# A two-layer encoder on one Trainium2 core: the split weights of each column block are placed at one of twelve odd shifts in their tiles

## The chip, the cores and the metric

The kernel runs on one core of one Trainium2 chip. The metric is the device time of one execution in microseconds (us), the median over runs. Five engines work side by side and meet only at semaphores: TensorE (PE, matrix products, with PEld for its weight loads), VectorE (DVE), ScalarE (ACT), GpSimd (POOL) and SyncE (SP, which here issues the weight transfers). On-chip memory (SBUF) has 128 partitions; a tile is a stretch of bytes at the same address in each of them.

## The reference, cut to what matters

256 tokens of 2048 channels pass through two residual layers.

```
layer 0: u = rmsnorm(h) @ w_in            # B, C, dt, x, z for a state-space branch; q, k, v, g for attention
         h += concat(ssd(z, x, B, C, dt), attention(q, k, v) * silu(g)) @ w_out
         h += sigmoid(rmsnorm(h) @ w_gate[0]) * (p[0] @ w_proj[0])
layer 1: a, a_gate, g = split(rmsnorm(h) @ w_od, 3)
         v = layernorm(depthwise_conv31(a * sigmoid(a_gate)))
         h += (silu(v) * silu(g)) @ w_odo
         h += sigmoid(rmsnorm(h) @ w_gate[1]) * (p[1] @ w_proj[1])
out = rmsnorm(h)
```

All weights and inputs are float32. The weights are read once, 333 MB in all, and nearly all of the arithmetic is in these products.

## The kernel before, in words

**Three products for one.** Each product is made from two parts of either operand: `hi`, the operand rounded to the type fp32r, and `lo`, the rest. `hi*hi + hi*lo + lo*hi` are three matmuls that add up in the same PSUM tile.

**Jobs.** All weights are cut into column blocks, mostly 512 columns wide, in the order in which they are used. `add` (line 156) appends a block to a list: its tensor, first row, number of 128-row slices, first column, width, the engine of the `lo` part (`low`) and a shift `at`. `Weights` cuts each block into jobs of two 128-row slices of 512 columns (four of 256). `emit` (lines 94 to 120) does for a job: one DMA on SP's queue into `raw` (512 KB); ACT writes `whi`, the fp32r copy (line 117); DVE, or POOL where `low` says so (layer 1's input projection but for its first two and last three blocks), writes `wlo = raw - whi` (line 119). `raw`, `whi` and `wlo` have four buffers each, and a job is emitted three ahead of its use (`take`, line 122).

**The shift.** A tile of `whi` or `wlo` has 1088 elements a partition, 1024 for the job and 64 spare (`SPARE`). `emit` uses the stretch `t[:, at:at + nk * ncols]`, so that the job's weights begin `at` elements, four bytes each, behind the tile's start. In the built program each of these tiles starts 160 bytes past a multiple of 256, and the operand tiles `ahi` and `alo` of the normalised input too (those of the two gate products, `xg`, 224 bytes past one, and those of the first `w_proj` product, `ph` and `pl`, 96 or 224). Blocks get `at=0` or the default 16 elements (64 bytes), so all weights begin 160 or 224 bytes past a multiple of 256.

**Two kinds of product.** In `proj` (lines 282 to 306) the weights are the stationary operand: a weight load (LDWEIGHTS) takes 128 columns of `whi` or `wlo`, and the 256 tokens of `ahi` or `alo` are streamed past them (moving operand, 256 columns). Lines 297, 298 and 299 are the three matmuls; I call this channel-major. In `proj_rows` (lines 315 to 332) the operand parts are stationary, 128 tokens at a time, and 512 columns of `whi` or `wlo` are streamed; lines 325, 326 and 327, token-major. Channel-major blocks have `at=16` (B, C, dt, x, q, k, g, and all of layer 1's input projection). Token-major blocks have `at=0` (first `w_proj`, z, v, `w_out`, `w_odo`), but for both `w_gate` and the second `w_proj`, which take the default 16. The last block of all, 256 columns of `w_gate[1]`, has `low=None`: it is split into operand tiles, without a shift (lines 984 to 994).

**The order of the work.** PE's order is as written: after each job's matmuls `pump` lets one step of the background work go in between (state-space groups, attention heads, transposes, the sums for norms). The other engines follow a scheduler, and PE waits for them by semaphores.

Of the kernel before, what the change touches and what calls it, by code (L numbers as in the profile page):

```python
# [45 lines left out]
OD_PAIRS = 2  # L46
NB = D // 512
SPARE = 64
SHIFT = 16
LAST_BLOCKS, LAST = [(0, 512), (512, 512), (1024, 512), (1536, 256)], (1792, 256)  # L50
LN_BLOCK, LN_STEP, LN_WAIT = 4, 9, 9
# [24 lines left out]
class Weights:  # L76
# [17 lines left out]
    def emit(self):  # L94
# [3 lines left out]
        def tile_(p, dt, n, spare=0, at=0):  # L98
            t = p.tile([P, G * 512 + spare], dt, name=f"{n}{i}", tag=n)
            return t[:, at:at + nk * ncols].rearrange("p (k c) -> p k c", c=ncols)  # L100
# [6 lines left out]
        if low is None:  # L107
# [7 lines left out]
            return  # L115
        hi, lo = (tile_(self.hl_pool, F32R, n, SPARE, at) for n in ("whi", "wlo"))
        self.high = nc.scalar.activation(hi, raw, AF.Copy)  # L117
# [11 lines left out]
def trunk(ctx, tc, t, out, dbg=None):  # L129
# [23 lines left out]
    w_odo = t["od_w_out"][0]  # L153
    jobs = []

    def add(w, k0, nk, c0, n, low=lambda i: False, at=SHIFT):
        jobs.append((w, k0, nk, c0, n, low, at))

    for c in range(NB):
        add(t["ple_w_proj"][0], 0, 2, 512 * c, 512, at=0)  # L160
    for o in (O_B, O_C):
        for j in range(2):
            add(w_in, 0, KT, o + 512 * j, 512)
    add(w_in, 0, KT, O_DT, 64)
    for j in range(4):
        add(w_in, 0, KT, O_X + 512 * j, 512)
        add(w_in, 0, KT, O_Z + 512 * j, 512, at=0)
    for j in range(4):
        for o in (O_Q, O_K, O_V, O_G):
            add(w_in, 0, KT, o + 512 * j, 512, at=0 if o == O_V else SHIFT)  # L170
    for kh in range(2):
# [857 lines left out]
def _build(arrays, dbg_names=None):  # L1029
    import concourse.bacc as bacc  # L1030
    nc = bacc.Bacc("TRN2", target_bir_lowering=False, num_devices=1)
    t = {}
    for name, a in arrays.items():
        t[name] = nc.dram_tensor(f"in_{name}_dram", a.shape, mybir.dt.from_np(a.dtype), kind="ExternalInput").ap()
    out = nc.dram_tensor("out_0_dram", (1, T, D), F32, kind="ExternalOutput").ap()
    dbg = None
    if dbg_names is not None:
        def dbg(name, ap):
            d = nc.dram_tensor(f"dbg_{name}", tuple(ap.shape), F32, kind="ExternalOutput").ap()
            nc.sync.dma_start(d, ap)  # L1040
            dbg_names.append(name)
    with tile.TileContext(nc) as tc:
        trunk(tc, t, out, dbg=dbg)
    return nc
# [8 lines left out]
```

## Time and profile before

| what | value |
|---|---|
| runs of the kernel | 1854.61 and 1862.58 us, median 1858.59 |
| the profiled execution | 1848.71 us, its span 1847.0 us |
| granted TensorE clock, mean over the span | 0.992 |
| DMA | 339.38 MB, 184 GB/s over the span |
| channel-major matmuls (lines 297 to 299) | 8,496 |
| token-major matmuls (lines 325 to 327) | 3,168, of which 3,072 have 512 columns and 96 have 256 |

How to read it: a matmul's duration in the profile goes from its start to the modelled end of its pipeline, so that durations overlap. The rate of PE is the step from one matmul's start to the next one's. With an undisturbed stream the two go together: where the step is 113.3 ns the duration is 276 ns, at 117.8 it is 281, at 120.0 it is 283, and at 226.7 (512 columns) it is 389, always some 163 ns more than the step. A mean duration of a group is so a measure of its rate.

### The profile page before, as it was taken

How to read it: one execution, taken by the hardware profiler on the slowest of the kernel's cores; microseconds unless marked ns; L12 is line 12 of the kernel's file. 1: busy time of each engine (PE TensorE's matmuls, PEld its weight loads, DVE VectorE, ACT ScalarE, POOL GpSimd, SP SyncE). 2: the span in 40 equal slices, each digit the busy share in tenths (PEclk: the TensorE clock that was granted, in tenths of full speed). 3: DMA queues.
4: the chain of work that ended last, by engine and by line, in shares of the span. 5: the costliest groups of instructions: out<-in, count | busy, mean ns of one | idle time of the engine just before them, and what ended most of it. 6: DMA issues, size and time to landing. Idle time of an engine off the chain costs nothing.

```text
span 1847.0 us, 31810 instructions
## 1 busy us (share of the span) xinstructions
PE 1812.9 (98%) x12532; PEld 1675.7 (91%) x12532; DVE 1308.2 (71%) x2160; ACT 947.5 (51%) x1312; POOL 649.3 (35%) x392
## 2 busy tenths in 40 slices
PE   7999999999999999999999999999999999999998
PEld 6999899889999999888888999999999999788887
DVE  6777876854656566665555688998899978765565
ACT  4555555544444455544555644444445447444454
POOL 2003876730000000000000399999999945100011
PEclk8999999999999999999999999999999999999999
DMA  7666445446666666565555476666666655566554
GB/s 259 195 174 193 126 149 158 150 142 193 183 187 183 188 172 196 178 224 193 183 187 189 145 220 196 194 190 190 192 205 194 194 156 167 193 203 202 187 183 137
DMA packets 192758, 339.38 MB, mean 184 GB/s; under 512 B 25408, under 2 KB 38208, under 8 KB 192480
## 3 DMA queue, kind: packets, MB, share of 16 engines
q1 hardware_dynamic: 190880, 332.23, 58.5%
q10 hardware_dynamic: 1104, 2.88, 0.4%
q8 instruction: 98, 1.61, 0.3%
q0 software_dynamic: 624, 2.24, 0.3%
q14 instruction: 52, 0.43, 0.1%
HBM read 333.11 MB, written 4.19 MB: 183 GB/s over the span
## 4 chain that ended last, share of the span: by engine, by line
PE 88%; DVE 6%; POOL 2%; DMA 1%; issue 1%; ACT 1%; SPq 0%; DVEq 0%; POOLq 0%; ACTq 0%
PE acc L297 16%; PE acc L298 16%; PE acc L299 16%; PE acc L325 12%; PE acc L327 12%; PE acc L326 12%; DVE wlo L119 2%; DMA raw<-in_ple_w_proj_dram 1%; PE htp L435 1%; DVE xsg L555 1%; POOL segr L582 1%; PE ya L655 1%; ACT whi L117 1%; DVE vc L904 1%; DVE lnsq L911 0%
## 5 line engine op out<-in xcount | busy, mean ns | idle before, releaser
L117 ACT ACTIVATE whi<-raw 128x1024 fp32r<-128x1024 f32 (+1 forms) x633 | 653.5, 1034 | 694.3 <-PE acc L298 328.0
L119 DVE TENSOR_TENSOR wlo<-raw,whi 128x1024 fp32r<-128x1024 f32 (+1 forms) x465 | 580.2, 1251 | 378.8 <-ACT whi L117 377.6
L299 PE MATMUL acc<-ahi,wlo 128*128 128x256 f32 (+1 forms) x2832 | 786.8, 278 | 3.8 <-DVE wlo L119 2.3
L297 PE MATMUL acc<-ahi,whi 128*128 128x256 f32 (+1 forms) x2832 | 790.3, 279 | 0.0
L298 PE MATMUL acc<-alo,whi 128*128 128x256 f32 (+1 forms) x2832 | 786.6, 278 | 1.8 <-DVE alo L340 1.8
L299 PEld LDWEIGHTS acc<-ahi,wlo 128*128 128x128 f32 (+1 forms) x2832 | 533.3, 188 | 4.7 <-DVE wlo L119 2.9
L298 PEld LDWEIGHTS acc<-alo,whi 128*128 128x128 f32 (+1 forms) x2832 | 534.7, 189 | 3.0 <-DVE alo L340 2.3
L297 PEld LDWEIGHTS acc<-ahi,whi 128*128 128x128 f32 (+1 forms) x2832 | 533.3, 188 | 1.3 <-DVE d L507 0.2
L119 POOL TENSOR_TENSOR wlo<-raw,whi 128x1024 fp32r<-128x1024 f32 (+1 forms) x168 | 383.6, 2298 | 55.2 <-ACT whi L117 54.0
L325 PE MATMUL acc<-whi,ahi 128*128 128x512 f32 (+1 forms) x1024 | 399.2, 390 | 2.5 <-DVE q4l L337 2.5
L327 PE MATMUL acc<-whi,alo 128*128 128x512 f32 (+1 forms) x1024 | 396.8, 387 | 2.3 <-DVE alo L337 2.3
L326 PE MATMUL acc<-wlo,ahi 128*128 128x512 f32 (+1 forms) x1024 | 396.1, 387 | 0.0
L870 DVE SCALAR_TENSOR_TENSOR cacc<-vc,vecs,cacc 128x249 f32<-128x249 f32 (+14 forms) x960 | 376.9, 473 | 10.2 <-ACT cacc L867 7.3
L373 POOL TENSOR_TENSOR rh<-rh,nhalf 128x2 f32<-128x2 f32 x4 | 2.8, 700 | 799.7 <-DVE rh L372 799.6
L327 PEld LDWEIGHTS acc<-whi,alo 128*128 128x128 f32 x1024 | 192.8, 188 | 43.1 <-DVE alo L337 3.5
L325 PEld LDWEIGHTS acc<-whi,ahi 128*128 128x128 f32 x1024 | 192.8, 188 | 39.8 <-DVE q4l L337 2.8
L326 PEld LDWEIGHTS acc<-wlo,ahi 128*128 128x128 f32 x1024 | 192.9, 188 | 37.7
L582 POOL TENSOR_SCALAR_AFFINE_SELECT dm<-dt_tok 128x512 f32<-128x512 f32 x32 | 38.5, 1207 | 130.3 <-DVE dt_tok L530 127.5
L339 ACT ACTIVATE ahi<-htp,vecs 128x256 fp32r<-128x256 f32 x64 | 29.0, 466 | 37.6 <-DVE alo L340 31.7
L340 DVE SCALAR_TENSOR_TENSOR alo<-htp,vecs,ahi 128x256 fp32r<-128x256 f32 x64 | 30.0, 480 | 13.1 <-ACT ahi L339 13.0
L954 POOL TENSOR_TENSOR hw<-h,wf 128x512 f32<-128x512 f32 (+1 forms) x8 | 13.4, 1669 | 67.2 <-DVE h L950 28.4
L890 POOL TENSOR_TENSOR vc<-vc,sg 128x512 f32<-128x512 f32 x8 | 31.3, 3951 | 10.1 <-ACT vc L888 10.1
(227 smaller groups left out, 1234.5 us busy)
## 6 DMA issues: line engine op xcount, KB each, us to landing
raw<-in_ev_w_in_dram SPq DMA_DIRECT2D x225, 512.0 KB, 3.8
raw<-in_od_w_in_dram SPq DMA_DIRECT2D x176, 512.0 KB, 4.4
raw<-in_ev_w_out_dram SPq DMA_DIRECT2D x64, 512.0 KB, 3.6
raw<-in_od_w_out_dram SPq DMA_DIRECT2D x64, 512.0 KB, 3.8
raw<-in_ple_w_gate_dram SPq DMA_DIRECT2D x60, 512.0 KB, 3.6
raw<-in_od_w_in_dram SPq DMA_DIRECT2D x32, 256.0 KB, 2.8
raw<-in_ple_w_proj_dram SPq DMA_DIRECT2D x8, 512.0 KB, 5.2
braw<-in_ev_rpb_dram SPq DMA_DIRECT2D x32, 96.0 KB, 6.6
```

Of the source, the lines that this page charges most:

```text
L117: self.high = nc.scalar.activation(hi, raw, AF.Copy)
L119: self.low = eng.tensor_sub(lo, raw, hi.bitcast(F32))
L297: nc.tensor.matmul(o, lhsT=hi[:, kk, cs], rhs=mh, start=st, stop=False, skip_group_check=True)
L298: nc.tensor.matmul(o, lhsT=hi[:, kk, cs], rhs=ml, start=False, stop=False, skip_group_check=True)
L299: nc.tensor.matmul(o, lhsT=lo[:, kk, cs], rhs=mh, start=False, stop=sp_, skip_group_check=True)
L325: nc.tensor.matmul(acc[c], lhsT=mh[:, ts_], rhs=hi[:, kk, :], start=k == 0, stop=False)
L326: nc.tensor.matmul(acc[c], lhsT=mh[:, ts_], rhs=lo[:, kk, :], start=False, stop=False)
L327: nc.tensor.matmul(acc[c], lhsT=ml[:, ts_], rhs=hi[:, kk, :], start=False, stop=k == nk - 1)
L340: b = nc.vector.scalar_tensor_tensor(lo, src, scale, hi.bitcast(F32), op0=ALU.mult, op1=ALU.subtract)
L582: nc.gpsimd.affine_select(out=out, in_=src[:, :, None].to_broadcast([P, 4, P]), pattern=[[0, 4], [pat, P]], compare_op=ALU.is_ge, fill=0.0 ...
L870: nc.vector.scalar_tensor_tensor(accs[b][:, c, lo_:hi_], av[b][:, c, lo_ + s:hi_ + s], w, accs[b][:, c, lo_:hi_], op0=ALU.mult, op1=ALU.add)
L890: (nc.gpsimd if i % 2 else nc.vector).tensor_tensor(vc[i], vc[i], sg[i], op=ALU.mult)
```

## The change

Two tables are new, and `add` no longer uses the shift that its caller gives, but only whether that was zero. The blocks that had 0 take the next place in `ROWS_AT`, all others the next in `CHAN_AT`, each list with a counter of its own that goes round.

```
+CHAN_AT = (12, 20, 14, 18, 15, 17, 4, 28, 36, 44, 52, 60)
+ROWS_AT = (4, 60, 2, 62, 1, 63, 12, 20, 28, 36, 44, 52)
...
+    count = [0, 0]
+
     def add(w, k0, nk, c0, n, low=lambda i: False, at=SHIFT):
+        kind = int(at == 0)
+        places = (ROWS_AT if kind else CHAN_AT)
+        at = places[count[kind] % len(places)]
+        count[kind] += 1
         jobs.append((w, k0, nk, c0, n, low, at))
```

The shifts count elements: 12 is 48 bytes, 15 is 60, 1 is 4. None is a multiple of 8 elements (32 bytes). In order of use the blocks get:

| blocks | shift in elements |
|---|---|
| first `w_proj`, 4 blocks | 4, 60, 2, 62 |
| B, C (two blocks each), dt | 12, 20, 14, 18, 15 |
| x and z, four times in turn | x 17, 4, 28, 36; z 1, 63, 12, 20 |
| q, k, v, g, four times | q, k, g: 44, 52, 60; 12, 20, 14; 18, 15, 17; 4, 28, 36; v 28, 36, 44, 52 |
| `w_out`, 8 blocks | 4, 60, 2, 62, 1, 63, 12, 20 |
| `w_gate[0]`, second `w_proj` (token-major, from `CHAN_AT`) | 44, 52, 60, 12; 20, 14, 18, 15 |
| layer 1, gate and value columns, 18 blocks (the first four 256 wide) | 17, 4, 28, 36, 44, 52, 60, 12, 20, 14, 18, 15, 17, 4, 28, 36, 44, 52 |
| layer 1, g columns, 8 blocks | 60, 12, 20, 14, 18, 15, 17, 4 |
| `w_odo`, 8 blocks | 28, 36, 44, 52, 4, 60, 2, 62 |
| `w_gate[1]`, 4 blocks (the last 256 wide) | 28, 36, 44, 52 |

Tiles, sizes, buffers, instructions and their order on each engine and the semaphores are the same as before; only the addresses at which `whi` and `wlo` are written and read differ. Line numbers behind the tables move by 3, behind `add` by 9.

## The prediction

> **What bounds the kernel now.** I read the page first: the busy shares, the chain of waits, the costliest groups.
>
> ```profile
> PE 1812.9 (98%) x12532; PEld 1675.7 (91%) x12532; DVE 1308.2 (71%) x2160; ACT 947.5 (51%) x1312; POOL 649.3 (35%) x392
> ...
> PE 88%; DVE 6%; POOL 2%; DMA 1%; issue 1%; ACT 1%; SPq 0%; DVEq 0%; POOLq 0%; ACTq 0%
> ...
> L299 PE MATMUL acc<-ahi,wlo 128*128 128x256 f32 (+1 forms) x2832 | 786.8, 278 | 3.8 <-DVE wlo L119 2.3
> L297 PE MATMUL acc<-ahi,whi 128*128 128x256 f32 (+1 forms) x2832 | 790.3, 279 | 0.0
> L298 PE MATMUL acc<-alo,whi 128*128 128x256 f32 (+1 forms) x2832 | 786.6, 278 | 1.8 <-DVE alo L340 1.8
> ```
>
> PE works 98% of the span, 88% of the chain is PE, and in the largest groups it waits 3.8 us or less. So the time is the number of matmuls times the step from one start to the next. The change keeps the number and alters where the weights lie. What has to be known is whether the step depends on that place.
>
> It does already, by three views of the same 256-column matmul. First, groups within single blocks: the last C block (channel-major, weights 224 past a multiple of 256, operand 160), the g block of attention's second round (the same places), the 256-column block of the last gate product (token-major, both 224), and the closing block in operand tiles (moving 160, stationary 224):
>
> ```profile
> L299 PE MATMUL acc<-ahi,wlo 128*128 128x256 f32 x64 | 17.7, 276 | 0.0
> ...
> L297 PE MATMUL acc<-ahi,whi 128*128 128x256 f32 x64 | 18.0, 281 | 0.0
> ...
> L326 PE MATMUL acc<-wlo,ahi 128*128 128x256 f32 x30 | 8.5, 283 | 0.0
> ...
> L992 PE MATMUL acc<-ahi,ahi 128*128 128x256 f32 x32 | 8.8, 276 | 0.0
> ```
>
> The last two have the same size and roles and differ in the moving operand's address: 283 against 276 ns. In starts (timeline; first and last row of a stretch, 183 steps in the first, 186 in the second, 84 in the third):
>
> ```profile
> 102.92 0.28 PE L297 MATMUL acc<-ahi,whi 128*128 128x256 f32 x1
> ...
> 123.66 0.28 PE L297 MATMUL acc<-ahi,whi 128*128 128x256 f32 x1
> ...
> 528.08 0.28 PE L297 MATMUL acc<-ahi,whi 128*128 128x256 f32 x1
> ...
> 549.98 0.28 PE L297 MATMUL acc<-ahi,whi 128*128 128x256 f32 x1
> ...
> 1815.89 0.28 PE L325 MATMUL acc<-whi,ahi 128*128 128x256 f32 x1
> ...
> 1825.97 0.28 PE L325 MATMUL acc<-whi,ahi 128*128 128x256 f32 x1
> ```
>
> 20.74 / 183 = 113.3 ns, 21.90 / 186 = 117.7, 10.08 / 84 = 120.0. So there are three levels. The C and g blocks show that one pair of places can run at two of them. What sets the level shows in the weight loads, of the g block and of the 256-column block:
>
> ```profile
> L298 PEld LDWEIGHTS acc<-alo,whi 128*128 128x128 f32 x64 | 12.3, 192 | 0.0
> L299 PEld LDWEIGHTS acc<-ahi,wlo 128*128 128x128 f32 x64 | 12.0, 188 | 0.0
> ...
> L326 PEld LDWEIGHTS acc<-wlo,ahi 128*128 128x128 f32 x30 | 5.8, 192 | 0.0
> L327 PEld LDWEIGHTS acc<-whi,alo 128*128 128x128 f32 x30 | 5.8, 192 | 0.0
> ```
>
> In the g block one load in three takes 4 ns more, in the 120-ns block every load. A load runs while the matmul before it streams; I read this as the two readers of SBUF getting in each other's way, more or less by their places and the phase between them.
>
> The token-major 512-column matmuls: `w_odo` (both operands 160 past a multiple of 256) and the second block of the first `w_proj` (weights 160, operand 96 or 224), then the first v block at half clock:
>
> ```profile
> 1595.19 0.39 PE L327 MATMUL acc<-whi,alo 128*128 128x512 f32 x1
> ...
> 1614.91 0.39 PE L327 MATMUL acc<-whi,alo 128*128 128x512 f32 x1
> ...
> 13.05 0.39 PE L325 MATMUL acc<-whi,ph 128*128 128x512 f32 x1
> ...
> 15.12 0.39 PE L325 MATMUL acc<-whi,ph 128*128 128x512 f32 x1
> ...
> 409.15 0.63 PE L326 MATMUL acc<-wlo,ahi 128*128 128x512 f32 x1
> ...
> 411.71 0.63 PE L326 MATMUL acc<-wlo,ahi 128*128 128x512 f32 x1
> ```
>
> 19.72 / 87 = 226.7 ns; 2.07 / 9 = 230.0, 3.3 more; 2.56 / 6 = 426.7 at clock 0.50. Half of that would be 213.3, so at full clock the stream pays 13.3 ns, 6%, that it does not pay at half clock.
>
> **The change part by part.** Nothing is removed or added; the instructions and their order are the same on every engine, so no transfer moves and no queue changes. Two kinds of access get new addresses.
>
> *Channel-major weight loads.* 44 blocks of 192 matmuls (512 columns' worth), plus the short dt block, which I leave out. 15.5 of them get 14, 15, 17 or 18 elements, within 8 bytes of today's 16: I leave them at today's level. 28.5 get a multiple of 4 (12, 20, 4, 28, 36, 44, 52, 60), 16 bytes or more away. No row has such a place. The bounds are the levels: 276 ns (no loss) and 283 (a loss of 6.7 ns). I take 281, a loss of 4.5: it is the middle level, and the one to which channel-major blocks fall when their loads are disturbed. Two of the 28.5 (g of rounds one and four) are there already, and eight (x, q and k) are so in part, as the second q block shows:
>
> ```profile
> L297 PE MATMUL acc<-ahi,whi 128*128 128x256 f32 x64 | 17.8, 278 | 0.0
> L298 PE MATMUL acc<-alo,whi 128*128 128x256 f32 x64 | 17.7, 277 | 0.0
> ```
>
> some 1.5 ns. So 26.5 x 192 x 4.5 ns = 22.9 us, less 8 x 192 x 1.5 ns = 2.3 us: **20.6 us**. At 283 it would be 26.5 x 192 x 6.7 - 2.3 = 31.8 us. The bound below zero: were every disturbance gone, the mean of the three big groups, 278.3, would fall to 276, at most 8,496 x 2.3 ns = 20 us; but that mean holds the half-clock matmuls too, and of what is sure, the four g blocks, there are 4 x 192 x 4.5 ns = 3.5 us. I keep 10 us as the low end.
>
> *Token-major streams.* 31 blocks of 96 matmuls. Eight get 1, 2, 62 or 63, next to today's 0 in the 64-element round, and stay. 23 get a multiple of 4, or stand in the gate and leave 16. Their nearest row is the 230.0: 96 x 3.3 ns = 0.32 us a block, 23 x 0.32 = **7.4 us**; the low bound is nothing. The 256-column gate block is at 120.0 already and keeps it.
>
> *The writes.* ACT's `whi` and DVE's `wlo` go to the new addresses. Where DVE writes, PE waits only 2.3 us for it. I cost this at nothing on ACT and DVE; POOL is a rival below.
>
> Sum: 20.6 + 7.4 = 28 us. On the profiled execution, 1848.7, this is 1876.7. That execution is 9.9 us below the median of the two runs shown, 1858.6; the new median is judged against the latter, so I give 1858.6 + 28 = **1887 us**.
>
> **The rivals.** *No effect.* If SBUF is read in pieces that a shift within 32 bytes does not change in number, the streams are as before, and only the phase is redrawn. For it: blocks 64 bytes apart, `w_odo` at 0 and the gate at 16, have the same 389 ns. Against it: 276 against 283 above. The time would be 1858.6, give or take 8. [...]
>
> *The 6% doubles for odd starts.* If a start off the 32-byte grid makes the reader fetch a further piece as often as it does now, the token-major step grows by 13.3 ns: 31 x 96 x 13.3 ns = 40 us, 1899; with the channel-major loads also held up to 120.0 in all blocks, 44 x 192 x 6.7 - 3.5 = 53 us more, 1952. I call it 1925. For it: the 6% goes with the clock, so reading is close to its limit. Against: no start in the trace is off 32 bytes. It decides where token-major durations pass 396 ns in whole blocks.
>
> *POOL becomes the bound in layer 1's input projection.* There POOL writes `wlo`, one tile for 24 matmuls (the whole run, then 1052 to 1380 us):
>
> ```profile
> L119 POOL TENSOR_TENSOR wlo<-raw,whi 128x1024 fp32r<-128x1024 f32 (+1 forms) x168 | 383.6, 2298 | 55.2 <-ACT whi L117 54.0
> ...
> L119 POOL TENSOR_TENSOR wlo<-raw,whi 128x1024 fp32r<-128x1024 f32 x115 | 274.7, 2404 | 23.9 <-ACT whi L117 23.2
> ```
>
> 24 x 113.3 = 2.72 us against 2.40. From 13% slower on, POOL sets the pace; at a quarter slower, 3.0 us, some 160 full tiles x 0.28 = 45 us, 1903. For it: POOL has the least slack of the writers. Against: nothing shows that it minds the place.
>
> *Faster: odd starts lose the 6%.* If the 6% is a meeting of the two readers that 16 bytes of offset avoid, token-major steps fall to 213.3: 31 x 96 x 13.3 = 40 us less, 1819, and half of the blocks would give 1839. Against: the closing block and the channel-major ones pay the same 6% with other places, and so does dt, whose loads are shorter (134 ns against 188):
>
> ```profile
> L297 PEld LDWEIGHTS acc<-ahi,whi x2832: 134/188/333, 29.3 to 1568.8; 128*128 128x128 f32 x188, 128*64 128x64 f32 x1
> ```
>
> so it looks like the stream's own. [...]
>
> **How the numbers follow.** Forecast (other levels) 0.45, its own range 1870 to 1906; no effect 0.28; the doubled 6% 0.14; POOL 0.05; faster 0.08. The range goes from 1848 (10 us below the median: the low end of channel-major) to 1925: all 44 blocks at 283 (53 us) and all 31 at 230.0 (10 us) give 1922, and the middle of the doubled 6% is just beyond. About 2% is what a measurement of this kernel can tell from no change: 1821 and 1896. Slower by more: 0.13 of the forecast's 0.45, 0.14 and 0.05, so 0.32. Faster by more: 0.03, under half of that rival. Within 2%: 0.65.
>
> **What would show it.** Each block of the changed kernel is one shift, so its profile is a table: 276, 281 or 283 ns by shift for channel-major, 389 to 393 for token-major. Right if 12, 20 and the other multiples of 4 stand at 281 or more with loads of 190 and up in layer 1's long stretch (1052 to 1380 us), where all is 276 now, while 14 to 18 stay. Wrong in place if 15 and 17 lose as much; wrong altogether if that stretch stays at 276, or if POOL's `wlo` passes 2.7 us. If token-major durations fall under 380, the sign is wrong.

## The result and the profile after

The changed kernel takes 1891.67 us (1890.25 and 1893.09), against 1858.59 before. The ratio is 1.0237, with a 95% interval from 1.0207 to 1.0268: slower by 2.4%. The profiled execution has a span of 1888.5 us, 41.5 more than the 1847.0 of before. The ratio is not the quotient of the two medians, which is 1.018. It corresponds to some 1848 us before, close to the profiled 1848.71, and the runs behind it are not on record. In 13 and in 23 later runs beside the experiments the kernel before had a median of 1849.06 us both times, and by that the change costs 43 us, not 33. Of these 36 runs 27 took 1843.9 to 1851.7 us and nine 1864.9 to 1869.2, and as none of the nine was profiled, it is open whether they are due to the second step of a place that is found below.

The page of the changed kernel (lines 306 to 308 are the old 297 to 299, 334 to 336 the old 325 to 327, 122 the old 119):

```profile
PE 1858.2 (98%) x12532; PEld 1710.5 (91%) x12532; DVE 1308.6 (69%) x2160; ACT 947.4 (50%) x1312; POOL 634.1 (34%) x392
...
PE 90%; DVE 6%; DMA 1%; issue 1%; ACT 1%; POOL 1%; SPq 0%; DVEq 0%; POOLq 0%; ACTq 0%
...
L306 PE MATMUL acc<-ahi,whi 128*128 128x256 f32 (+1 forms) x2832 | 801.9, 283 | 0.0
L308 PE MATMUL acc<-ahi,wlo 128*128 128x256 f32 (+1 forms) x2832 | 799.0, 282 | 2.1 <-DVE wlo L122 2.1
L307 PE MATMUL acc<-alo,whi 128*128 128x256 f32 (+1 forms) x2832 | 798.7, 282 | 1.9 <-DVE alo L349 1.9
...
L334 PE MATMUL acc<-whi,ahi 128*128 128x512 f32 (+1 forms) x1024 | 403.8, 394 | 2.5 <-DVE q4l L346 2.5
L336 PE MATMUL acc<-whi,alo 128*128 128x512 f32 (+1 forms) x1024 | 400.8, 391 | 1.4 <-DVE alo L346 1.4
L335 PE MATMUL acc<-wlo,ahi 128*128 128x512 f32 (+1 forms) x1024 | 401.2, 392 | 0.0
L122 POOL TENSOR_TENSOR wlo<-raw,whi 128x1024 fp32r<-128x1024 f32 (+1 forms) x168 | 368.6, 2210 | 88.1 <-ACT whi L120 86.2
```

DVE and ACT work as long as before, POOL a little less, the waits of the big groups are as small as they were, and PE is busy 45 us longer with the same 12,532 matmuls. The matmuls that read the shifted tiles take some 4 ns longer on the average, in every group.

By block, in groups of the changed kernel at shifts 14 and 15 (channel-major), 52 (channel-major), then 1, 63 and 36 (token-major):

```profile
L306 PE MATMUL acc<-ahi,whi 128*128 128x256 f32 x64 | 18.0, 281 | 0.0
...
L307 PE MATMUL acc<-alo,whi 128*128 128x256 f32 x64 | 18.1, 283 | 0.0
...
L306 PE MATMUL acc<-ahi,whi 128*128 128x256 f32 x64 | 17.8, 278 | 0.0
...
L335 PE MATMUL acc<-wlo,ahi 128*128 128x512 f32 x32 | 12.8, 401 | 0.0
...
L336 PE MATMUL acc<-whi,alo 128*128 128x512 f32 x32 | 12.5, 390 | 0.0
...
L334 PE MATMUL acc<-whi,ahi 128*128 128x512 f32 x32 | 12.7, 396 | 0.0
```

and the weight loads of the block at 14:

```profile
L306 PEld LDWEIGHTS acc<-ahi,whi 128*128 128x128 f32 x63 | 11.9, 189 | 0.0
L308 PEld LDWEIGHTS acc<-ahi,wlo 128*128 128x128 f32 x63 | 11.9, 189 | 0.0
L307 PEld LDWEIGHTS acc<-alo,whi 128*128 128x128 f32 x63 | 11.8, 188 | 0.0
```

No channel-major block is left at 276, where most stood before, and the shifts next to 16 lose as much as the others. The loads are hardly longer than the 187.7 ns that they took in the blocks of before at 276.

The mean step of a block, from the matmuls' starts (steps of over 150 ns in channel-major blocks, at half clock or around other work, left out), by shift, in ns. Channel-major blocks of layer 1, beside them what the first experiment below gives with nothing else running:

| shift | 4 | 12 | 14 | 15 | 17 | 18 | 20 | 28 | 36 | 44 | 52 | 60 |
|---|---|---|---|---|---|---|---|---|---|---|---|---|
| changed kernel | 118.3 | 117.8 | 117.8 | 119.5 | 118.3 | 118.3 | 118.7 | 120.0 | 118.4 or 120.0 | 118.1 | 116.7 | 117.3 or 120.0 |
| matmuls alone | 118.3 | 117.8 | 117.8 | 119.8 | 118.3 | 118.2 | 118.7 | 120.0 | 120.0 | 118.2 | 116.7 | 119.9 |

Summed over all blocks, steps times matmuls grew by 37.2 us (channel-major) and 15.9 (token-major), the lengths of the blocks by 30.7 and 9.8. The difference, some 13 us, is in the long steps that are left out of the means (in token-major blocks those over 300 ns): they sum to 50.8 us before and to 37.9 us after. So time in which PE had waited or run at half clock gave way to longer steps; the mean clock was 0.992 before and 0.996 after.

### The profile page after: what moved, and what is told of

Same layout as the page of the kernel before. It is cut to its first block, busy times and chain, and to the rows that moved or that the text cites. A ratio compares the mean times of both kernels' runs of the same rounds, so it can differ in the third digit from the quotient of the medians.

```text
span 1888.5 us, 31810 instructions
## 1 busy us (share of the span) xinstructions
PE 1858.2 (98%) x12532; PEld 1710.5 (91%) x12532; DVE 1308.6 (69%) x2160; ACT 947.4 (50%) x1312; POOL 634.1 (34%) x392
## 4 chain that ended last, share of the span: by engine, by line
PE 90%; DVE 6%; DMA 1%; issue 1%; ACT 1%; POOL 1%; SPq 0%; DVEq 0%; POOLq 0%; ACTq 0%
PE acc L306 17%; PE acc L307 17%; PE acc L308 17%; PE acc L334 12%; PE acc L335 12%; PE acc L336 12%; DVE wlo L122 2%; DMA raw<-in_ple_w_proj_dram 1%; PE htp L444 1%; DVE xsg L564 1%; PE ya L664 1%; ACT whi L120 1%; DVE vc L913 1%; PE seg L644 0%; DVE lnsq L920 0%
## 5 line engine op out<-in xcount | busy, mean ns | idle before, releaser
L306 PE MATMUL acc<-ahi,whi 128*128 128x256 f32 (+1 forms) x2832 | 801.9, 283 | 0.0
L308 PE MATMUL acc<-ahi,wlo 128*128 128x256 f32 (+1 forms) x2832 | 799.0, 282 | 2.1 <-DVE wlo L122 2.1
L307 PE MATMUL acc<-alo,whi 128*128 128x256 f32 (+1 forms) x2832 | 798.7, 282 | 1.9 <-DVE alo L349 1.9
L334 PE MATMUL acc<-whi,ahi 128*128 128x512 f32 (+1 forms) x1024 | 403.8, 394 | 2.5 <-DVE q4l L346 2.5
L335 PE MATMUL acc<-wlo,ahi 128*128 128x512 f32 (+1 forms) x1024 | 401.2, 392 | 0.0
L122 POOL TENSOR_TENSOR wlo<-raw,whi 128x1024 fp32r<-128x1024 f32 (+1 forms) x168 | 368.6, 2210 | 88.1 <-ACT whi L120 86.2
L335 PEld LDWEIGHTS acc<-wlo,ahi 128*128 128x128 f32 x1024 | 193.3, 189 | 41.3
L591 POOL TENSOR_SCALAR_AFFINE_SELECT dm<-dt_tok 128x512 f32<-128x512 f32 x32 | 34.6, 1083 | 133.9 <-DVE dt_tok L539 131.1
L866 DVE TENSOR_TENSOR vc<-acc,sg 128x512 f32<-128x512 f32 x16 | 11.1, 691 | 44.3 <-PE acc L308 44.1
L963 POOL TENSOR_TENSOR hw<-h,wf 128x512 f32<-128x512 f32 (+1 forms) x8 | 13.3, 1668 | 68.6 <-DVE h L959 29.0
```

The lines of the kernel that those rows point to most:

```text
L122: self.low = eng.tensor_sub(lo, raw, hi.bitcast(F32))
L306: nc.tensor.matmul(o, lhsT=hi[:, kk, cs], rhs=mh, start=st, stop=False, skip_group_check=True)
L307: nc.tensor.matmul(o, lhsT=hi[:, kk, cs], rhs=ml, start=False, stop=False, skip_group_check=True)
L308: nc.tensor.matmul(o, lhsT=lo[:, kk, cs], rhs=mh, start=False, stop=sp_, skip_group_check=True)
L334: nc.tensor.matmul(acc[c], lhsT=mh[:, ts_], rhs=hi[:, kk, :], start=k == 0, stop=False)
L335: nc.tensor.matmul(acc[c], lhsT=mh[:, ts_], rhs=lo[:, kk, :], start=False, stop=False)
```

## The experiments

Theory A: the step is set by the places of the weight load and of the stream relative to each other, as the two readers meet. Theory B: an odd start costs by itself. Theory C: the writes to odd places cost.

### Matmuls alone

A kernel of its own, which leaves the computation of the reference out, loads one block of `x`, makes two stationary tiles `wt` and two moving tiles `mv` in fp32r, all 160 bytes past a multiple of 256, and then PE runs alone. `ws` is the shift of the load and `ms` that of the stream, in elements; a set is 36 matmuls with one pair of shifts:

```
def run(ws, ms, n, cols=P, reps=12):
    for r in range(reps):
        o = acc[r % 2][:cols, :n]
        for i, (w, m) in enumerate(((0, 0), (0, 1), (1, 0))):
            nc.tensor.matmul(o, lhsT=wt[w][:, ws:ws + cols], rhs=mv[m][:, ms:ms + n], start=i == 0, stop=i == 2)
    spacer()            # one float32 matmul of 128 columns
...
for s in SHIFTS: run(s, 0, 256)
for s in SHIFTS: run(0, s, 512)
for s in SHIFTS: run(0, s, 512, 16)
for s in SHIFTS: run(16, s, 256)
for s in DIAG: run(16 + s, s, 256)
for s in DIAG: run(s, s, 512)
```

> This kernel leaves the whole computation of the reference out: it only issues weight loads and matmuls on two small pairs of fp32r tiles, with nothing else running, 36 matmuls for each pair of places, both tiles beginning 160 bytes past a multiple of 256. Theory A (the two readers meet: the step depends on where the weight load reads relative to the stream): with the stream fixed at 0 and the load moved, 256 columns, 16 elements give 113.3 ns or 117.8 and nearly all other shifts 116.7 to 120; with the load fixed at 0 and the stream moved, 512 columns, 0 gives 226.7 and the others 228 to 238, as in the changed kernel; with a load of only 16 columns the 512-column step loses most of its dependence, within 2 ns of one value at all shifts; and moving both by the same odd amount (pairs 16+s with s, 256 columns) gives back the step of the pair 16 with 0 to within 1.5 ns. Theory B (an odd start costs by itself, in the reader that has it): the short load changes nothing in the dependence on the stream's shift, and moving both by the same amount is the worst case, as both starts are odd. Theory C (the cost comes from ACT's, DVE's and POOL's writes to odd places): no dependence at all here, as nothing writes: 113.3 and 226.7 everywhere.

The timeline (start, length, count) of the sets with the load at 13, 15, 16, 28, then the stream at 0 and 1, the stream at 0 and 8 with loads of 16 columns, both at 8 and both at 1, and last the load at 16 with the stream at 18:

```profile
70.86 4.39 PE L54 MATMUL acc<-mv,wt 128*128 128x256 f32 x36
...
79.71 4.54 PE L54 MATMUL acc<-mv,wt 128*128 128x256 f32 x36
84.23 4.34 PE L54 MATMUL acc<-mv,wt 128*128 128x256 f32 x36
...
119.62 4.57 PE L54 MATMUL acc<-mv,wt 128*128 128x256 f32 x36
...
164.50 8.45 PE L54 MATMUL acc<-mv,wt 128*128 128x512 f32 x36
172.93 8.76 PE L54 MATMUL acc<-mv,wt 128*128 128x512 f32 x36
...
456.59 8.59 PE L54 MATMUL acc<-mv,wt 128*16 128x512 f32 x36
...
525.25 8.42 PE L54 MATMUL acc<-mv,wt 128*16 128x512 f32 x36
...
1001.07 8.44 PE L54 MATMUL acc<-mv,wt 128*128 128x512 f32 x36
...
958.13 8.81 PE L54 MATMUL acc<-mv,wt 128*128 128x512 f32 x36
...
829.10 4.76 PE L54 MATMUL acc<-mv,wt 128*128 128x256 f32 x36
```

A set that runs through at 113.3 ns takes 4.34 us, at 120.0 4.57; at 226.7 it is 8.42 to 8.46, at 237 to 238 8.76 to 8.81. The set with the load at 13 lies between, as it takes some ten matmuls to come down to 113.3. The second row of the table above is from here: shift by shift the steps of the changed kernel, within 0.3 ns at ten of twelve. Of the other places of the load 13, 19 and 22 stand at 113.3, as 16 does.

**Theory C** is out, as nothing writes here and the loss is whole.

**Theory A.** Half of it holds: with both moved by 8, 16, 24 or 32 elements 512 columns run at 226.7 again, where the stream moved alone gives 228.9 to 233.3. The other half does not: both moved by 1, 2, 3 or 6 stay at 228.8 to 237.8. With 256 columns and the pair 16 and 0 moved together the step is 113.3 at 4, 12 and 24, 117.8 at 8, 16 and 32, and 116.7 to 120.0 at 1, 2, 3 and 6, where A expected 113.3 within 1.5 throughout. And the short load, which should have taken the dependence away, only redraws it, from 226.7 to 237.8. So it is not that the stream suffers while a load lasts.

**Theory B** alone does not hold either: the stream moved by 8, 24 or 32 is on the 32-byte grid and loses 6 ns. The largest loss found is the load at 16 with the stream at 18, 256 columns: 126.7 ns, 13 more than the best.

### The two tables apart, and a sweep on the 32-byte grid

```
+        if not kind:             # channel_only; "if kind:" in rows_only
             at = places[count[kind] % len(places)]
...
+CHAN_AT = ROWS_AT = (0, 8, 16, 24, 32, 40, 48, 56)      # multiples_of_8, instead of both tables
```

> The new shifts only in the blocks that had 16 (channel-major, and the token-major gates and second w_proj); the blocks that had 0 keep it. From the steps of the changed kernel's blocks the channel-major part is 37 us of matmul steps, of which some 31 us show in the lengths of the blocks. Theories A and B: 24 to 32 us above the kernel before, 1883 to 1891, and the sum of this run's and the next run's differences is the whole change's 33 us within 6. If the phase at which one block leaves the next one matters (the blocks disturb each other), the sum is off by more than 6 us.

> The new shifts only in the blocks that had 0 (first w_proj, z, v, w_out, w_odo); all others keep 16. Theories A and B: token-major steps of those blocks go from 227 to 228 to 238 ns as in the changed kernel, some 25 blocks x 96 x 5 ns = 12 us at the most, 6 to 12 us above before: 1864 to 1871.

> Both tables hold 0, 8, 16, 24, 32, 40, 48, 56: places on the 32-byte grid only, every block the next one. Theory A (relation of the two places): shift by shift different levels on the grid too; channel-major 16 at 113.3 or 117.8, others between 113.3 and 120; token-major 0 at 226.7 and others to 232; the time between before and the change, 1862 to 1885. Theory B (only a start off the 32-byte grid costs): all blocks as before, 113.3 to 117.8 and 226.7, 1850 to 1862.

Beside 1849.06 us: 1880.93 with the channel table alone (ratio 1.0156, 1.0110 to 1.0202), 1858.49 with the row table alone (1.0041, 1.0019 to 1.0064). From median to median that is 31.9 and 9.4 us, 41.3 together, and the whole change costs 42.6 by the same base: they add up. Both differences are as expected; the absolute times are not, and neither is the sum of 33, as both had been counted from 1858.6. The sweep on the grid takes 1889.46 (1.0196, 1.0140 to 1.0252), at the change's level and above what I expected. That settles B: places on the 32-byte grid cost as much. By shift, channel-major: 0, 120.0 ns; 8, 118.3; 24, 117.3; 40, 120.0. The surprise was 16: with the same places as before, its blocks in layer 1 stood at 117.8, between blocks of other shifts, where they had been at 113.3. The first of them:

```profile
L306 PE MATMUL acc<-ahi,whi 128*128 128x256 f32 x63 | 17.7, 281 | 0.0
```

So the step is not a matter of the two places alone.

### Does a pair of places have one step?

The same kind of kernel, `run(s, 0, 256)` sixteen times for each place, after spacers of 8 to 128 columns (`spacer(c)` instead of `spacer()`).

> Again only weight loads and matmuls, with the whole computation of the reference left out. First part: for six places of the load (13, 16, 19, 22, 48, 52 elements, the stream at 0, 256 columns) 36 matmuls after each of sixteen interruptions of different length (one float32 matmul of 8 to 128 columns); second part the same after six 512-column matmuls; third part the stream at 0, 7, 15 in 512 columns; last the load at 21 places with the stream at 0 in 512 columns, with loads of 128 and of 16 columns. Theory A2 (one pair of places has more than one lasting step, and the phase at entry picks it): 16 settles at 113.3 after some interruptions and at 117.8 after others, within the same pair of places; the places that ran at 113.3 in the grid split into some that always return to 113.3 and some that do not; 52 always 116.7. Theory A1 (the places alone set the step): every place gives one value after all entries. On the load: if the two readers meet only while a load lasts, the short load makes the step independent of the load's place, within 2 ns; if it is the place at which the load begins or the moment of its start, the short load depends on its place as much as the long one, 226.7 to 238.

Timeline of the first sets with the load at 16, the first two at 19, and two at 13, late in its row:

```profile
82.32 4.49 PE L56 MATMUL acc<-mv,wt 128*128 128x256 f32 x36
86.79 4.35 PE L56 MATMUL acc<-mv,wt 128*128 128x256 f32 x36
91.11 4.49 PE L56 MATMUL acc<-mv,wt 128*128 128x256 f32 x36
95.58 4.35 PE L56 MATMUL acc<-mv,wt 128*128 128x256 f32 x36
...
152.64 4.34 PE L56 MATMUL acc<-mv,wt 128*128 128x256 f32 x36
156.96 4.34 PE L56 MATMUL acc<-mv,wt 128*128 128x256 f32 x36
...
50.49 4.57 PE L56 MATMUL acc<-mv,wt 128*128 128x256 f32 x36
55.04 4.57 PE L56 MATMUL acc<-mv,wt 128*128 128x256 f32 x36
```

The steps in which the sixteen sets end: at 16, 113.3 eight times and 117.8 eight times; at 13, 113.3 nine times, then 120.0 seven times; at 19, 113.3 always; at 22, 113.3 five times and 116.7 eleven times; at 48, 117.8 always, but 113.3 after five of six sets of 512-column matmuls; at 52, 116.7 always. At 13, 16 and 22 sets behind 512-column matmuls ended at 113.3 five, five and six times of six. So a pair of places has one or two lasting steps, and the way in picks one (A2). For 512 columns with the stream at 0, 7 and 15 all 48 sets ended at 226.7. In the last part 512-column steps depend on the load's place with loads of 128 columns (226.7 at 0, 230.0 to 234.6 elsewhere) and of 16 (226.7 to 235.6). The dependence stays with the short load, but the good places are others: 4 elements give 226.7 with the short load and 233.3 with the long one.

### Another single place

These start from the kernel before. The token-major blocks that had the default keep 16, but for the last one, 256 columns wide, which goes to 0 (119.9 to 117.8 ns, 0.2 us in all).

```
-SHIFT = 16
+SHIFT = 19        # or 22, 13
...
-        add(t["ple_w_gate"][0], 0, KT, 512 * c, 512)
+        add(t["ple_w_gate"][0], 0, KT, 512 * c, 512, at=16)      # second w_proj likewise
...
-        add(t["ple_w_gate"][1], 0, KT, c0, n)
+        add(t["ple_w_gate"][1], 0, KT, c0, n, at=16 if n == 512 else 0)
```

> All channel-major weights at 22 elements instead of 16, one place for the whole kernel; token-major blocks as before, but for the last, 256-column gate block, at 0 instead of 16. If 22 always settles at 113.3: the blocks that stand at 117.8 before (g, parts of x, q, k) gain, up to 7 us, and the 256-column block 0.6 us: 1842 to 1848 where before is 1849. If an odd start costs by itself: 116 to 120 in all channel-major blocks, 1870 to 1890.

> The same with 19 elements, which is off the 8-byte grid too. If places alone decide: 113.3 as in the grid, 1842 to 1849. If an odd start costs by itself: 1870 to 1890.

> The same with 13 elements. If places alone decide: 113.3 as in the grid, 1842 to 1849. If an odd start costs by itself: 1870 to 1890.

19 takes 1841.49 us against 1849.06, ratio 0.9947 (0.9921 to 0.9972); 22 takes 1841.90, 0.9946 (0.9907 to 0.9985); 13 takes 1886.58, 1.0188 (1.0145 to 1.0231). All twelve runs of 19 (1839.70 to 1842.51) are faster than each of the 36 of before; of the twelve of 22 one took 1865.80, and that one was not profiled. The g block of attention's second round with 19, and a block of layer 1 with 13:

```profile
L297 PE MATMUL acc<-ahi,whi 128*128 128x256 f32 x45 | 12.4, 276 | 0.0
L298 PE MATMUL acc<-alo,whi 128*128 128x256 f32 x45 | 12.4, 276 | 0.0
```

```profile
L297 PE MATMUL acc<-ahi,whi 128*128 128x256 f32 x43 | 12.2, 284 | 0.0
L299 PE MATMUL acc<-ahi,wlo 128*128 128x256 f32 x42 | 11.9, 283 | 0.0
```

19 is odd, 12 bytes past a 32-byte boundary, and is the best place found for these loads: every g block of attention falls from 117.8 to 113.4 ns. With 13 the undisturbed B and C blocks stand at 120.0, the first x block is back at 113.4, and from the first g block of attention to the fifth of layer 1 the undisturbed blocks are at 120.0 again; the last one is at 113.3. The expectation for 13 by places alone missed; that pair has two steps, and which one a kernel gets was not to be read from the first table. Nor is it to be read from the counts of entries: 22 ended at 116.7 in eleven of sixteen sets, and in the kernel its undisturbed blocks stand at 113.3 but for the last g block of layer 1, at 116.7; 13 ended at 113.3 in nine of sixteen.

### Widths and bf16

Matmuls alone again, `for n in range(64, 513, 64): run(ws, ms, n)` for six pairs, then the same with bf16 tiles, moved in steps of their two-byte elements.

> Weight loads and matmuls alone, the reference's computation left out. Six pairs of places (load and stream at 0 and 0, 16 and 0, 19 and 0, 28 and 0, 0 and 1, 0 and 8 elements), each with streams of 64 to 512 columns in steps of 64; then bf16 tiles, the load at fifteen places with 256 columns and the stream at fifteen places with 512. If the loss of a bad pair is per matmul (a matter of the hand-over from one matmul to the next): the step above 17/16 of the columns at full clock is within 0 to 11 ns at every width, no more at 512 than at 256. If it is per column (a slower stream): it doubles from 256 to 512, from 6.7 to 13 ns for 28 and 0. If the 6% is part of the rate at which four-byte elements stream, the bf16 steps lack it, 107 to 110 ns for 256 columns and 213 to 217 for 512, and at all places the same within 2 ns; if it belongs to the matmuls in general, bf16 has 113.3 and 226.7 too and depends on its places as much.

Timeline of the pair 28 and 0 at 192 to 512 columns, and of bf16 at 256 and 512:

```profile
176.87 4.24 PE L64 MATMUL acc<-mv,wt 128*128 128x192 f32 x36
181.12 4.56 PE L64 MATMUL acc<-mv,wt 128*128 128x256 f32 x36
185.65 5.53 PE L64 MATMUL acc<-mv,wt 128*128 128x320 f32 x36
191.16 6.64 PE L64 MATMUL acc<-mv,wt 128*128 128x384 f32 x36
197.78 7.59 PE L64 MATMUL acc<-mv,wt 128*128 128x448 f32 x36
205.34 8.64 PE L64 MATMUL acc<-mv,wt 128*128 128x512 f32 x36
...
315.45 4.09 PE L64 MATMUL acc<-mb,wb 128*128 128x256 bf16 x36
319.60 4.09 PE L64 MATMUL acc<-mb,wb 128*128 128x256 bf16 x36
...
377.75 7.93 PE L64 MATMUL acc<-mb,wb 128*128 128x512 bf16 x36
```

The best steps, 113.3 and 226.7, are in proportion to the columns; I take the same proportion, as an estimate from these two, for the best step of the widths between, which no set reached. From 256 columns on the loss over it is 3 to 12 ns wherever a pair loses, with no growth in the width: 7 ns at 256 and 6.7 at 512 for this pair. So it is paid per matmul. A pair that is good at one width need not be at another: 19 and 0 lose nothing at 256 and 6.9 ns at 512, 0 and 0 lose 6.7 at 256 and nothing at 512. At 192 columns and less the step stays at 111.7 ns, wherever the clock was full. So it is not the width that sets it there; what does was not shown, as no run varies the load at these widths. bf16 runs at 109.2 ns at all fifteen places of the load and at 215.8 to 216.7 at all places of the stream.

## Why the prediction was right, and where it was not

The sign, the mechanism (the step of the matmuls that read the shifted tiles, and nothing else) and the range were right. The size was low: I took 28 us, and the profile shows 41.5; that 1887 lies so near to 1891.67 is luck, owed to the median of 1858.6, which was 9.5 us high. The most likely outcome, a time within 2% of before at a chance of 0.65, did not come by the ratio of 1.0237.

By the steps the sum was further off than by the time. The steps grew by 53 us where I had 28, and some 13 us of that went into time in which PE had waited or run at half clock. I had taken each ns of step as time, and had no term for this.

- **Middle level for 28.5 channel-major blocks (20.6 us).** Right in kind. They stand at 116.7 to 120.0, 117.8 was in the middle, and their steps grew by 24.9 us. The signs were drawn too finely: 12, 20, 52 and 60 have blocks of 278 to 280 ns, under my 281.
- **The 15.5 blocks at 14, 15, 17 and 18 stay (nothing).** Wrong in place, by the sign that I had given for it, and the term that was missing: they stand at 117.8 to 119.5, and their steps grew by 12.2 us. Two reasons are shown. Another place four bytes away can have another step: matmuls alone give 119.8 and 118.3 at 15 and 17. And 113.3 was not the level of 16 but one of its two steps: the sweep on the grid has 16 itself at 117.8. The C and g blocks had shown both, and I still took a place to have one level.
- **Token-major, 3.3 ns for 23 blocks and nothing for eight (7.4 us).** Mis-sized: the row of the nine steps at the start was too low a guide. The 23 blocks grew by 11.5 us, some 5 ns a matmul, and the eight near ones by 4.3 (1 element: 9 to 11 ns a matmul); only the two at 63 and the first of `w_odo`, at 28, stayed within 1.5 ns.
- **The reading of the loads.** I read the 192 ns in the slow blocks as the loads being held up, and expected 190 and more. They are 187 to 190 in nearly all blocks at 117.8 to 120, and a load of 16 columns leaves the dependence. Here the duration of a load is no guide to the level.
- **No effect.** Out: the matmuls that read the shifted tiles step mostly 2 to 11 ns longer, at places on the 16-byte grid as well (12 elements, 48 bytes: 117.8 ns, where layer 1's blocks stood at 113.3).
- **The doubled 6%.** Its sign came, and the rival did not: token-major durations pass 396 ns in whole blocks (401 at 1 element), but the step grew by 11 ns at the most, not 13.3, and on the 32-byte grid, where this rival has no loss, `w_out` stands at 233 too. The sign was drawn too low to tell the two apart.
- **POOL, a faster stream.** Neither came. POOL's tile fell from 2298 to 2210 ns in a slower stage, and no undisturbed block has a step under 113.3 or 226.7.

What stays open is the inside: why the loss of a pair is what it is, and how the entry picks between two steps. The runs show what it is not: no other engine (matmuls alone step by 113.3 ns with the load at 16 and by 120.0 at 28), nothing that a shorter load takes away (226.7 to 237.8 with loads of 16 columns), no column rate (7 ns at 256 columns, 6.7 at 512), no alignment of one operand alone (512 columns stand at 226.7 with both moved by 8, 16, 24 or 32, and at 228.9 to 233.3 with the stream alone moved as far).

## What to carry to other kernels

Where a profile is PE nearly throughout and operands are fp32r, compare the duration of equal matmuls block by block: two levels 2 to 6% apart in one group are time (here durations of 276 and 281 to 283 ns, steps of 113.3 and 117.8 to 120.0), and the address of an operand may be what tells them apart. A sweep that gives each block another address measures many places in one run, but a pair of places may hold two steps (the load at 16: 113.3 and 117.8), and only the whole kernel at one place tells which it gets. A place that returned to the low step after every entry is the safe choice (here 19 elements: 113.3 ns after all sixteen spacers, and a time 0.4% below the median of before), not one that has been seen there once. Measure it at the width that the kernel uses: 19 is good for 256 columns (113.3 ns) and not for 512 (6.9 ns over 226.7).

## What the runs showed of the hardware that was not expected

- At full clock an fp32r matmul steps by 113.3 ns for 256 columns and 226.7 for 512 at the best. At half clock the kernel before steps by 213.3 and 426.7, half of which is 106.7 and 213.3: so at full clock there are 6% more. bf16 has 109.2 and 215.8.
- A bad pair of places adds up to 13 ns per fp32r matmul (126.7 for 256 columns), with no growth in the width. bf16 showed nothing of it at fifteen places of the load (109.2 ns) and fifteen of the stream (215.8 to 216.7).
- Some pairs of places have two lasting steps: 113.3 and 117.8 ns (the load at 16), 113.3 and 120.0 (13), or 113.3 and 116.7 (22). In the undisturbed blocks of the profiled kernels none changed from one to the other.
- Four bytes can cost or gain 5 ns in 113: the load at 18, 19 and 20 elements gave 118.2, 113.3 and 118.7.
